# A hybrid attention and mLSTM layer: state products of both directions in one split product, value blocks in pairs

## The chip, the cores and the metric

The kernel runs on one core of one Trainium2 chip. The metric is device time in microseconds (us) of one execution. A core has five engines with queues of their own: PE (TensorE, matrix products), DVE (VectorE), ACT (ScalarE), POOL (GpSimd) and SP (SyncE, which here only issues DMAs). Loading PE's stationary matrix is listed apart as PEld. A queue is worked off in order, so an instruction that waits holds up all that stand behind it on its engine.

## The reference

One layer over T = 2048 tokens of width 1024, in float32. What matters here:

```python
proj = h @ w_in + b_in          # na_q na_k na_v na_z, ml_q ml_k ml_v ml_o ml_z, gates
na_out = neighbourhood_attention(na_q, na_k, na_v, rpb) * silu(na_z)
mq, mk = split(silu(short_conv(concat(ml_q, ml_k))))
# chunked mLSTM, one head, forward (the backward direction is the same on flipped input)
m_new = max(bl_c + m, max(a_c)); decay = exp(bl_c + m - m_new); w = exp(a_c - m_new)
C_new = decay * C + einsum('s,se,sd->ed', w, v_c, k_c)     # state product
n_new = decay * n + einsum('s,sd->d', w, k_c)              # its normaliser
...
y = concat([na_out, ml_out]) @ w_out; out = rmsnorm(x + gate * y)
```

There are 4 mLSTM heads of width 128. The kernel uses 16 chunks of 128 tokens.

## The kernel before

**Split products.** Float32 factors of the large products are written as a high part (rounded to the matrix unit's single-pass format, `F32R`) and a low part, the rest. Three products stand for one: high x high, high x low, low x high. `mm3` (lines 635 to 640) does this over 8 slices of the contraction, so 24 matmuls make one tile. Small products, those of the mLSTM among them, are made in plain float32; the profile shows each as two PE records.

**Stages in order.**
1. `start` (hand-ordered with `manual_schedule`): modulation, normalisation, splitting of h; blocks 0 and 1 of the projection (value and output gate of heads 0 and 1), and the first token group of block 2.
2. `tok_blocks` (775 to 796): blocks 2 and 3 (heads 2 and 3) and 4 and 5 (na_v), each 256 columns wide, over four groups of 512 tokens, a group being four PSUM tiles of 128 tokens (`vo_group`, `nav_group`). The order is block by block. There are two weight slots (`wslot`), used by turns; `raw_w` loads the next block in two halves into `raw0` and `raw1`, ACT copies the high part, DVE makes the low part. After each tile `next(self.chain)` writes one step of the gate chain (`gate_both`, then `decays`), small dependent steps on DVE, ACT and PE. Bias rows lie in two `brows`, one for even and one for odd blocks, loaded by `load_bias`.
3. `conv_blocks` (970): blocks 6 to 9 (ml_k, ml_q) with tokens in the columns, the short convolution on DVE, for k also a transpose on PE (lines 1043 to 1049); results go to `d_ck` in DRAM.
4. `phase1b`: per head `ml_pass1` (state products of the 16 chunks from both ends, and the recurrence `follow`) and `ml_pass2` (outputs). Between their steps `pump(n)` puts n matmuls of the generator `nq_gen` (line 1094: blocks 10 to 17, 512 columns). In `ml_pass1` a chunk is loaded as one `kv` tile (k turned, v, a column of ones), DVE multiplies v and the ones by the chunk's weights for each direction (line 1263), PE makes one 129-column product `dc` for each direction (line 1283), and DVE or ACT takes it up (1267, 1290, 1294). Five pumped matmuls on some steps and four on the others stand between chunks (`PUMP1` = 4.5). `ml_pass2` gathers four chunks in `hm` (two buffers), turns them on PE, multiplies them with the gate tile `zt` in place (`end`, 1405 to 1410) and stores `zt`.
5. `phase2` (hand-ordered): neighbourhood attention patch by patch and the output product (line 1676). Buffers `ring` are cleared by POOL (line 1748), tables are loaded into `tabs` (1557).

**Order.** Outside `start` and the patch loop of `phase2` a planner orders each engine's instructions from the program's order and its own estimate of times; semaphores are set by it. In the hand-ordered parts every engine's order is the program's. SP's is too: in the last round of `start` it issues, in this order, the two halves of block 2's weights, the store of block 0 (line 721), the last two fills `d_t<-big` (758) and the store of block 1 (721); then in `tok_blocks` the loads for the gate row (587, 590, 596), `rneg` and three fills `d_e<-big` (727, 731), the halves of block 3 (203) and its bias row (681).

Of the kernel before, what the change touches and what calls it, by code (L numbers as in the profile page):

```python
# [58 lines left out]
class Kernel:  # L59
# [30 lines left out]
    def scratch(self):  # L90
        d = self.dram
        self.d_vna = d.tile([T, 512], F32, name="d_vna")
        self.d_ck = d.tile([MH, NC, P, 897], F32, name="d_ck")
# [41 lines left out]
    def phase1(self):  # L135
# [14 lines left out]
        wb = self.pool(r1a, "wb", bufs=1, side="right")  # L150
        self.wslot = []
        for nm, pl in (("a", wa), ("b", wb)):
            self.wslot.append(tuple(pl.tile([P, KT, 272 if nm == "a" else 256], F32R, name=f"w{part}_{nm}") for part in ("hi", "lo")))
# [18 lines left out]
        self.tok_blocks(self.pool(toks, "chain", bufs=1, side="right"))  # L172
# [16 lines left out]
    def stage_tile(self, name):  # L189
        self.stages.reverse()  # L190
        return self.stages[1].tile([P, 1032], F32, tag="st", name=name).rearrange("p (o c) -> p o c", o=4)

    def load_w(self, blk, slot, halves=(0, 1)):
        for part in self.raw_w(blk, slot, halves):
            part()

    def raw_w(self, blk, slot, halves=(0, 1)):
        nc = self.nc
        hi, lo = self.wslot[slot]

        def part(half):
# [11 lines left out]

        return [part(half) for half in halves]

    def start(self, left):
# [310 lines left out]
        def next_w():  # L527
            for part in self.raw_w(2, 0):
                yield
                part(nc.vector)  # L530

        fills = self.table_fills()
        self.chain = iter(())
# [132 lines left out]
    def nav_group(self, blk, slot, g):  # L666
        nc = self.nc
        c0 = (blk - 4) * 256
        st = self.stage_tile(f"stv_{blk}_{g}")
        for o in range(4):  # L670
# [3 lines left out]
            next(self.chain, None)  # L674
            if o == 1:
                self.flush()
        dst = self.d_vna[g * GT : (g + 1) * GT, c0 : c0 + 256].rearrange("(o p) c -> p o c", p=P)
        self.defer(lambda: nc.sync.dma_start(dst, st[:, :, :256]))
# [17 lines left out]
    def vo_group(self, h, slot, g, first=None, brow=None, tops=(), stage=None):  # L696
# [5 lines left out]
        for o in range(4):  # L702
# [10 lines left out]
            next(self.chain, None)  # L713
            if o == 1:
                self.flush()
        nc.scalar.activation(st[:, :, 129:257], st[:, :, 129:257], AF.Sigmoid)
        dst = self.d_ck[h, 4 * g : 4 * g + 4, :, 128:385].rearrange("o p c -> p o c")
        if g == 0 and h < 3:
            (nc.scalar if h == 0 else nc.sync).dma_start(dst, st[:, :, 0:257])
        else:  # L720
            self.defer(lambda: nc.sync.dma_start(dst, st[:, :, 0:257]))

# [52 lines left out]
    def tok_blocks(self, chain_pool):  # L775
        self.wide = chain_pool.tile([P, 2 * D], F32, name="wide")
        self.chain = itertools.chain(self.gate_both(chain_pool), self.decays(chain_pool))
        order = [2, 3, 4, 5]
        next(self.chain)
        r = self.tables_begin(chain_pool)  # L780
        for n, blk in enumerate(order):
            parts = self.raw_w(blk + 1, (blk + 1) % 2)
            if blk < 5:
                self.load_bias(blk + 1)
            for g in range(1 if blk == 2 else 0, NG):
                if blk < 4:
                    self.vo_group(blk, blk % 2, g)
                else:
                    self.nav_group(blk, blk % 2, g)
                if g in (1, 2):  # L790
                    parts[g - 1](self.nc.vector)
                if blk == 2 and g == 3:
                    self.tables_bias(r)
# [4 lines left out]
    def gate_chain(self, pool, gates):  # L798
# [29 lines left out]
        nc.scalar.activation(a, a, AF.Ln, bias=1.0)  # L828
        lf = new("lf")
# [78 lines left out]
    def decays(self, pool):  # L908
# [20 lines left out]
        def raised(n):  # L929
# [5 lines left out]
            dst = self.d_ck[h, 4 * gi : 4 * gi + 4, :, 641 + d * CH : 641 + (d + 1) * CH].rearrange("c p t -> p c t")  # L935
# [87 lines left out]
    def conv_group(self, pool, u, kind, ct, g):  # L1023
# [14 lines left out]
        dst = self.d_ck[ct, 4 * g : 4 * g + 4, :, 385 + j * CH : 385 + (j + 1) * CH].rearrange("c p t -> p c t")  # L1038
# [7 lines left out]
        st = self.stage_tile(f"stk_{ct}_{g}")[:, :, 0:128]  # L1046
# [118 lines left out]
    def phase1b(self, left, right):  # L1165
# [30 lines left out]
        mls.close()  # L1196
        self.todo = []
        self.stacks = [pps, right, left]

    def close(self):  # L1200

        self.last_z()
# [258 lines left out]
    def phase2(self):  # L1461
# [405 lines left out]
        with self.tc.manual_schedule():  # L1867
            for m in range(len(patches) + 1):
                slot(m)
# [95 lines left out]
```

## Time and profile before

| | us |
|---|---|
| median of 3 runs (lowest, highest) | 1277.23 (1277.06, 1277.59) |
| the profiled execution | 1276.39 |
| its span, first to last instruction | 1274.5 |
| stage 2, blocks 2 to 5, PE at line 638 | 130.6 to 305.8 of the span |
| stage 3, convolution blocks | 305.8 to 491 |
| the four `ml_pass1`, first to last `dc` | 533 to 555, 625 to 648, 718 to 741, 812 to 834 |
| first table step of the patch loop (line 1598) | 927.96 |

How to read it: a row of a group view gives line, engine, operation, output<-input, shape and count, then busy time and mean duration. A timeline row gives start, duration, engine, line and operation, and in brackets how long the engine was idle before and what ended that. PE's matmuls overlap: a record of a 256-column matmul lasts 0.28 us while the next starts 0.12 us later, so costs on PE are taken from start to start.

### The profile page before, as it was taken

How to read it: one execution, taken by the hardware profiler on the slowest of the kernel's cores; microseconds unless marked ns; L12 is line 12 of the kernel's file. 1: busy time of each engine (PE TensorE's matmuls, PEld its weight loads, DVE VectorE, ACT ScalarE, POOL GpSimd, SP SyncE). 2: the span in 40 equal slices, each digit the busy share in tenths (PEclk: the TensorE clock that was granted, in tenths of full speed). 3: DMA queues.
4: the chain of work that ended last, by engine and by line, in shares of the span. 5: the costliest groups of instructions: out<-in, count | busy, mean ns of one | idle time of the engine just before them, and what ended most of it. 6: DMA issues, size and time to landing. Idle time of an engine off the chain costs nothing.

```text
span 1274.5 us, 22948 instructions
## 1 busy us (share of the span) xinstructions
PE 1264.4 (99%) x8168; PEld 1095.4 (86%) x8168; DVE 790.3 (62%) x2391; ACT 537.7 (42%) x1182; POOL 201.7 (16%) x368
## 2 busy tenths in 40 slices
PE   9999999999999999999999999999999999999997
PEld 8999999999888888888888888888877888888886
DVE  7875542213667664267777778777556766767664
ACT  6642425442334222123323323324357565565552
POOL 0000003440000000000001001000424331332541
PEclk9999999999999999999999999999999999999999
DMA  9999947996678764745757867746677755655551
GB/s 366 335 309 286 283 147 198 249 245 180 180 180 189 165 154 115 207 131 164 204 160 207 251 189 215 240 149 186 207 249 266 230 162 160 203 177 176 176 173 67
DMA packets 217082, 259.08 MB, mean 203 GB/s; under 512 B 23435, under 2 KB 163595, under 8 KB 216968
## 3 DMA queue, kind: packets, MB, share of 16 engines
q1 hardware_dynamic: 149542, 190.09, 52.1%
q0 software_dynamic: 13616, 37.28, 8.9%
q10 hardware_dynamic: 53810, 30.24, 8.4%
q8 instruction: 65, 1.06, 0.3%
q14 instruction: 49, 0.40, 0.1%
HBM read 173.05 MB, written 92.72 MB: 209 GB/s over the span
## 4 chain that ended last, share of the span: by engine, by line
PE 95%; DVE 2%; ACT 1%; issue 1%; DMA 0%; DVEq 0%; ACTq 0%
PE pq L1094 27%; PE y L1676 14%; PE pc L639 5%; PE pc L640 5%; PE pc L638 5%; PE pO L1633 4%; PE pT L1618 3%; PE pvo L638 3%; PE pvo L640 3%; PE pvo L639 3%; PE pS L1587 3%; PE pvo L693 3%; PE pv L640 2%; PE pv L639 2%; PE pv L638 2%; PE pi L1346 2%
## 5 line engine op out<-in xcount | busy, mean ns | idle before, releaser
L1094 PE MATMUL pq<-hhi,whi_a 128*128 128x512 f32 x512 | 208.4, 407 | 0.0
L1094 PE MATMUL pq<-hlo,whi_a 128*128 128x512 f32 x512 | 207.8, 406 | 0.0
L1094 PE MATMUL pq<-hhi,wlo_a 128*128 128x512 f32 x512 | 207.2, 405 | 0.0
L1368 POOL TENSOR_TENSOR hm<-hm,ck 128x128 f32<-128x128 f32 x64 | 28.2, 440 | 580.3 <-DVE hm L1367 541.0
L1094 PEld LDWEIGHTS pq<-hhi,wlo_a 128*128 128x128 f32 x512 | 96.8, 189 | 16.7 <-issue 0.2
L1094 PEld LDWEIGHTS pq<-hlo,whi_a 128*128 128x128 f32 x512 | 96.7, 189 | 16.1 <-issue 0.4
L1094 PEld LDWEIGHTS pq<-hhi,whi_a 128*128 128x128 f32 x512 | 96.8, 189 | 15.9
L1599 ACT ACTIVATE ring<-ring,mn 128x480 f32<-128x480 f32 (+5 forms) x128 | 75.9, 594 | 55.8 <-DVE mn L1598 55.8
L1620 ACT ACTIVATE ring<-pT 96x384 f32<-96x384 f32 (+3 forms) x128 | 65.8, 514 | 63.5 <-PE pT L1618 62.0
L1676 PE MATMUL y<-hhi,wlo_a 128*128 128x512 f32 (+1 forms) x272 | 87.0, 394 | 0.2 <-ACT y L1683 0.2
L1676 PE MATMUL y<-hhi,whi_a 128*128 128x512 f32 x256 | 86.2, 408 | 0.0
L1349 ACT ACTIVATE num<-px,gtile 128x129 f32<-128x129 f32 x120 | 38.7, 367 | 105.2 <-PE px L1344 91.5
L1522 POOL DMA_DIRECT2D v<-d_vna x158 | 78.7, 505 | 15.6 <-issue 4.4
L1618 PEld LDWEIGHTS pT<-ident,ring 128*128 128x128 f32 (+2 forms) x416 | 51.1, 136 | 19.2 <-ACT ring L1620 3.7
L1618 PE MATMUL pT<-ident,ring 128*128 128x128 f32 (+2 forms) x416 | 66.2, 272 | 0.0
L638 PE MATMUL pvo<-whi_b,hhi 128*128 128x256 f32 x224 | 63.6, 284 | 0.0
L1598 DVE CUSTOM_DVE_ANT_0 ring<-pS,tab 128x480 f32<-128x480 f32 (+5 forms) x128 | 61.9, 539 | 2.6 <-PE pS L1587 2.4
L640 PE MATMUL pvo<-whi_b,hlo 128*128 128x256 f32 x224 | 63.1, 282 | 0.0
L639 PE MATMUL pvo<-wlo_b,hhi 128*128 128x256 f32 x224 | 63.0, 281 | 0.0
L934 ACT ACTIVATE dec<-dec,gtile 128x128 f32<-128x128 f32 x128 | 41.3, 391 | 46.9 <-POOL dec L927 43.2
L673 DVE TENSOR_TENSOR stv<-pv,brow 128x256 f32<-128x256 f32 x32 | 13.6, 425 | 71.8 <-PE pv L640 71.8
L710 DVE TENSOR_TENSOR stvo<-pvo,brow 128x256 f32<-128x256 f32 x60 | 24.7, 418 | 50.7 <-PE pvo L640 40.0
(343 smaller groups left out, 3331.3 us busy)
## 6 DMA issues: line engine op xcount, KB each, us to landing
ck<-d_ck SPq DMA_DIRECT2D x64, 384.5 KB, 3.6
rawq<-in_w_main_dram SPq DMA_DIRECT2D x28, 512.0 KB, 5.2
raw<-in_w_main_dram SPq DMA_DIRECT2D x18, 512.0 KB, 6.2
kv<-d_ck SPq DMA_DIRECT2D x64, 128.5 KB, 3.0
dec<-d_mneg SPq DMA_DIRECT2D x32, 256.0 KB, 6.0
d_ck<-dec ACTq DMA_DIRECT2D x32, 256.0 KB, 6.9
qs<-d_qna SPq DMA_DIRECT2D x30, 256.0 KB, 3.9
xr<-in_x_p_dram POOLq DMA_DIRECT2D x15, 512.0 KB, 3.9
```

The costliest lines, as they stand in the source:

```text
L638: nc.tensor.matmul(ps, lhi(k), rhi(k), start=(k == 0), stop=False)
L639: nc.tensor.matmul(ps, lhi(k), rlo(k), start=False, stop=False)
L640: self.mark = nc.tensor.matmul(ps, llo(k), rhi(k), start=False, stop=(k == KT - 1))
L934: nc.scalar.activation(t[:, o, :], t[:, o, :], AF.Exp, bias=self.cols["g"][:, d, h, c : c + 1])
L1094: self.mark = nc.tensor.matmul(patch_ps(ps) if patch else ps, w, self.htok(h, g, k, patch), start=(k == 0 and n == 0), stop=(k == KT - 1 a ...
L1522: queue.dma_start(chunks[key][r * nkc : (r + 1) * nkc, :], rows[r])
L1598: nc.vector.tensor_tensor_reduce(pt[:, :nk], ps, tabs[ct][:, j * nk : (j + 1) * nk], 1.0, 3e38, ALU.add, ALU.min, mn)
L1599: nc.scalar.activation(pt[:, :nk], pt[:, :nk], AF.Exp, bias=mn, scale=-1.0, accum_out=sums[:, j : j + 1])
L1618: nc.tensor.transpose(ps[:cs, i, :], U[u][j][:, i * cs : (i + 1) * cs], self.ident)
L1620: nc.scalar.activation(t[:cs, :nch, :], ps[:cs, :nch, :], AF.Copy)
L1633: nc.tensor.matmul(po[j * HD : (j + 1) * HD, ct, :], v[:n, h * HD : (h + 1) * HD], pt[j][:n, i, :], start=(i == 0), stop=(i == nch - 1))
L1676: nc.tensor.matmul(y, m[:, k, :], w[k][:, cs], start=(k == 4 and n == 0), stop=(k == 3 and n == 2))
```

## The change

- **Pairs.** The weight slots become two halves of one pair of tiles (`wpair`). `pair_group` makes a tile of 512 columns from two value blocks at once. The order of stage 2 becomes (block, group) = (2,1), (3,0), pair (2,2), pair (2,3), (3,1), (4,0), pairs (4,1), (4,2), (4,3), (5,0); a pair is of blocks 2 and 3 or of 4 and 5. Block 3's raw halves are issued in `start`, each right behind the split of block 2's half. The split of a block lies within single groups (`splits`). Two more stage buffers. A pair tile takes two steps of the gate chain. `load_bias(3)` is written behind `tables_begin`.
- **State products.** The convolution stores k turned as a high and a low part (`d_ck` rows of 1025 instead of 897 values). ACT makes the high part of the weighted v, DVE the low part, for both directions side by side; PE makes three products of 258 columns. Chunks at the ends, which need one direction, get both.
- **Places.** The second weight slot stays allocated; `kv` tiles (seven places as before), `zt` and the four tables lie in it (`spare`). `end` writes to `hm` and stores `hm`. Ten `ring` buffers: two `hm` and eight of their own; DVE clears their columns from 256 on at the start of the patch loop. Table 3 is loaded after `close`.

```diff
 def tok_blocks
-        order = [2, 3, 4, 5]
         next(self.chain)
         r = self.tables_begin(chain_pool)
-        for n, blk in enumerate(order):
-            parts = self.raw_w(blk + 1, (blk + 1) % 2)
-            if blk < 5:
-                self.load_bias(blk + 1)
-            for g in range(1 if blk == 2 else 0, NG):
...
-                if g in (1, 2):
-                    parts[g - 1](self.nc.vector)
+        order = [(2, 1), (3, 0), (2, 2), (2, 3), (3, 1), (4, 0), (4, 1), (4, 2), (4, 3), (5, 0)]
+        both = ((2, 2), (2, 3), (4, 1), (4, 2), (4, 3))
+        self.load_bias(3)
+
+        def splits(rest, after):
+            for _ in range(rest):
+                yield
+            for part in self.parts:
+                part(self.nc.vector)
+                yield
+            if after:
+                self.parts = self.raw_w(*after)
+                if after[0] == 5:
+                    self.load_bias(4)
+                if after[0] == 6:
+                    self.load_bias(5)
+
+        turns = {0: (1, (4, 0)), 4: (0, (5, 1)), 5: (0, (6, 0)), 9: (0, None)}
...
 def start, next_w
-            for part in self.raw_w(2, 0):
+            self.parts = []
+            for half, part in enumerate(self.raw_w(2, 0)):
                 yield
                 part(nc.vector)
+                self.parts.append(self.raw_part(3, 1, half))
...
+    def pair_group(self, blk, g):
...
+        for o in range(4):
+            ps = self.pp.tile([P, GT], F32, tag="pp", name=f"p2_{blk}_{g}_{o}")
+            self.mm3(
+                ps.rearrange("p (a c) -> p a c", a=2),
+                lambda k: self.hhi[g][:, k, o * P : (o + 1) * P],
+                lambda k: self.hlo[g][:, k, o * P : (o + 1) * P],
+                lambda k: hi[:, :, k, :256],
+                lambda k: lo[:, :, k, :256],
+            )
+            for j, st in enumerate(sts):
...
+                next(self.chain, None)
+            next(self.mid, None)
...
 def gate_chain
         nc.scalar.activation(a, a, AF.Ln, bias=1.0)
+        yield
...
 def conv_group
-        st = self.stage_tile(f"stk_{ct}_{g}")[:, :, 0:128]
-        nc.scalar.activation(st, ps.rearrange("p (a q) -> p a q", a=4), AF.Copy, scale=KSCALE)
+        nc.scalar.activation(hi.bitcast(F32R), turned, AF.Copy, scale=KSCALE)
+        nc.vector.scalar_tensor_tensor(lo.bitcast(F32R), turned, KSCALE, hi, ALU.mult, ALU.subtract)
...
 def ml_pass1
-            t = tiles[k] = ml.tile([P, 257], F32, tag="kv", bufs=7, name=f"kv_{h}_{order[k]}")
+            half, i = divmod(k % 7, 5)
+            t = tiles[k] = self.spare(half, 1024 * half + 385 * i, 385)
...
-                nc.vector.tensor_scalar(sides[k][d], v, self.cols["w"][:, d, h, c : c + 1], None, ALU.mult)
+            hi, lo = sides[k] = [ml.tile([P, 2, 129], F32R, tag=f"w{e}", bufs=3, name=f"w{e}_{h}_{c}") for e in range(2)]
+            for d in range(2):
+                w = self.cols["w"][:, d, h, c : c + 1]
+                nc.scalar.activation(hi[:, d, :], v, AF.Copy, scale=w)
+                nc.vector.scalar_tensor_tensor(lo[:, d, :], v, w, hi[:, d, :].bitcast(F32), ALU.mult, ALU.subtract)
...
-            for d, w in sorted(sides[k].items()):
-                nc.tensor.matmul(dc[:, d, :129], kt, w, start=True, stop=True)
+            for n, (a, b) in enumerate(((khi, whi), (khi, wlo), (klo, whi))):
+                nc.tensor.matmul(dc, a, b, start=n == 0, stop=n == 2)
...
 def ml_pass2, end
-            nc.vector.scalar_tensor_tensor(z, ps, self.mlw[:, h : h + 1], z, ALU.mult, ALU.mult)
-            src = zt[gi]
+            src = hm[gi]
+            nc.vector.scalar_tensor_tensor(src.rearrange("p a q -> p (a q)"), ps, self.mlw[:, h : h + 1], z, ALU.mult, ALU.mult)
...
 def phase2
-        for t in ring[4:] + ring[:4]:
-            nc.gpsimd.memset(t, 0.0)
...
         with self.tc.manual_schedule():
+            for t in ring:
+                nc.vector.memset(t[:, 256:], 0.0)
```

138 lines of the change are left out of this document (86 added, 52 removed).

## The prediction

> **What bounds the kernel now.** First the page's head and chain of work, then the list of PE's waits.
>
> ```profile
> span 1274.5 us, 22948 instructions
> PE 1264.4 (99%) x8168; PEld 1095.4 (86%) x8168; DVE 790.3 (62%) x2391; ACT 537.7 (42%) x1182; POOL 201.7 (16%) x368
> PE 95%; DVE 2%; ACT 1%; issue 1%; DMA 0%; DVEq 0%; ACTq 0%
> PE pvo L436 <- ACT hhi L404: 1.2, 2, 0.8
> PE y L1676 <- DVE hlo L1569: 0.4, 1, 0.4
> ```
>
> The span lies within the profiled execution of 1276.39 us, itself 0.84 below the median of 1277.23. PE is 95% of the chain that ended last, and hardly ever waits: the longest wait in the list's rows shown is 0.8 us. So only PE time taken out counts, and new work on other engines costs what it makes PE wait.
>
> **The change part by part.** *Pairs.* From start to start of one line's records in a tile of 24:
>
> ```profile
> L638 PE MATMUL pv<-whi_a,hhi x128: 276/280/283, 215.0 to 260.0; 128*128 128x256 f32 x128
> L638 PE MATMUL pc<-hhi,whi_b x64: 390/393/404, 446.7 to 490.7; 128*128 128x512 f32 x64
> 491.53 41.70 PE pq L1094 x180
> 82.94 12.09 PE pvo L693 x96
> ```
>
> Block 4: 127 rounds of three in 45.0 us, 0.1181 each at 256 columns. Block 9: 63 rounds of three in 44.0, 0.2328 at 512; line 1094 gives 41.70/180 = 0.2317. Five pair groups x 4 tiles x 24 = 480 wide matmuls replace 960: 480 x (2 x 0.1181 - 0.2328 or 0.2317) = 1.6 or 2.2 us. I take 1.9. The split operand and columns in two runs are not seen to cost in line 1094's patches either.
>
> *State products.* Around one chunk on PE, and the record counts:
>
> ```profile
> 538.36 0.39 PE L1094 MATMUL pq<-hhi,wlo_a 128*128 128x512 f32 x1
> 538.59 0.38 PE L1283 MATMUL dc<-kv 128*128 128x129 f32 x2
> 538.81 0.39 PE L1283 MATMUL dc<-wv,kv 128*128 128x129 f32 x2
> 538.95 0.48 PE L1094 MATMUL pq<-hhi,whi_a 128*128 128x512 f32 x1
> 539.27 0.39 PE L1094 MATMUL pq<-hlo,whi_a 128*128 128x512 f32 x1
> L1283 PE MATMUL dc<-kv x128: 271/273/276, 533.1 to 834.1; 128*128 128x129 f32 x128
> L1283 PE MATMUL dc<-wv,kv x112: 275/275/276, 535.8 to 834.3; 128*128 128x129 f32 x112
> ```
>
> From 538.36 to 539.27 are 0.91 us with two wide matmuls (0.463) in them: both directions cost 0.447, one 0.223. 240 records are 120 products: 56 chunks with two and 8 with one. No row has 258 columns. Below it stands 256 (0.1181), above it 272 (12.09/96 = 0.1259), so three cost 0.354 to 0.378; by nearness 0.357. Gain 56 x (0.447 - 0.357) = 5.0, less 8 x (0.357 - 0.223) = 1.1: **3.9 us**, with the ends 2.6 and 4.1.
>
> The Trainium skill (TensorE: Matmul & The Clock Gate, Back-to-back issue gap) puts an isolated matmul's gap at N/2.4 + 2.5 ns. By it the pairs would give an estimated 1.2 us and the state products 5.7, and the forecast would be about 1271.8; the rows here show 8 to 10 ns more per matmul, and they decide.
>
> *What the planner must place in `ml_pass1`.*
>
> ```profile
> 648.55 0.47 DVE L1263 TENSOR_SCALAR kv<-kv,gtile 128x129 f32<-128x129 f32 x2
> 649.20 2.19 DVE L1267 SCALAR_TENSOR_TENSOR st<-st,gtile,st 128x129 f32<-128x129 f32 x8
> 658.39 0.63 ACT L1349 ACTIVATE num<-px,gtile 128x129 f32<-128x129 f32 x2 [3.74 <-PE px L1344]
> 718.00:743.00 25.00, 25.00 (x144) 21.56 (x143) 19.16 (x69) 8.93 (x23) 0.41 (x1) 1.00 0.79 224
> ```
>
> Per head DVE exchanges 30 weightings (0.24) for 32 low parts (0.27): 1.6 us more on 19.2 of 25 (the window's third column). ACT gets 32 high parts at some 0.3: 10 on 8.9. Both fit. Weights are made two chunks ahead, 2.8 us of pumped work, against ACT plus DVE of some 1.2. `kv` grows by half, with as many places. I take 0; without that cover it is the fourth rival.
>
> *Convolution, `hm`, patch loop.*
>
> ```profile
> 306.00:399.00 93.00, 93.00 (x427) 75.61 (x427) 61.54 (x123) 30.44 (x46) 0.00 (x0) 1.00 0.74 187
> L1137 DVE SCALAR_TENSOR_TENSOR qst<-pq,bcol,qst x24: 719/744/751, 668.3 to 967.0; 128x512 fp32r<-128x512 f32 x24
> 593.20 0.37 ACTq L1410 DMA_DIRECT2D d_mix<-zt  x1
> 596.08 0.29 DVE L1366 TENSOR_SCALAR hm<-num,r 128x128 f32<-128x128 f32 x1
> 908.02 3.37 POOL L1748 MEMSET ring<- 128x512 f32 x7
> 927.96 0.46 DVE L1598 CUSTOM_DVE_ANT_0 ring<-pS,tab 128x288 f32<-128x288 f32 x1 [2.18 <-PE pS L1587]
> ```
>
> 16 low parts of k at 0.74 are 12 us of DVE in a stretch of 93 of which 62 are taken, under PE's blocks: 0. `hm` is now freed by a store issued at 593.20, 2.9 us before its next write at 596.08; a landing later than that delays DVE, under a whole chunk of pumped work: 0, at worst some 0.5 at each of eight places. Ten half-width clears on DVE, at half of POOL's 3.37/7 some 2.4 us, fall into the 2.18 us that DVE idles before the first table step; PE has pumped work there: 0 to 0.5. Table 3 is wanted second to last: 0. The larger rows of `d_ck` move 8 MB on a queue that is not full in these stages.
>
> *The start of stage 2.* Here the change moves DMAs past each other on SP.
>
> ```profile
> 120.43 0.91 SPq L203 DMA_DIRECT2D raw<-in_w_main_dram  x2
> 122.65 9.32 SPq L758 DMA_DIRECT2D d_t<-big  x2
> 133.05 4.41 SPq L721 DMA_DIRECT2D d_ck<-stvo  x1
> 137.55 0.88 SPq L587 DMA_DIRECT2D cact<-in_small_dram  x1
> 143.05 2.63 SPq L731 DMA_DIRECT2D d_e<-big  x3
> 145.73 1.11 SPq L203 DMA_DIRECT2D raw<-in_w_main_dram  x2
> 127.00:159.00 32.00, 32.00 (x271) 31.59 (x271) 16.89 (x49) 13.38 (x16) 0.32 (x3) 1.00 1.01 285
> 130.63 1.21 DVE L208 TENSOR_TENSOR wlo_a<-raw,whi_a 128x1024 fp32r<-128x1024 f32 x1
> 152.56 1.22 DVE L208 TENSOR_TENSOR wlo_b<-raw,whi_b 128x1024 fp32r<-128x1024 f32 x1 [5.31 <-ACT whi_b L207]
> 151.47 1.06 ACT L207 ACTIVATE whi_b<-raw 128x1024 fp32r<-128x1024 f32 x1 [4.30 <-DMA raw<-in_w_main_dram]
> 143.26 0.21 ACT L588 ACTIVATE cact<-cact 128x8 f32<-128x8 f32 x1 [3.81 <-DMA cact<-in_small_dram]
> 130.63 0.28 PE L638 MATMUL pvo<-whi_a,hhi 128*128 128x256 f32 x1
> ```
>
> Block 3's second raw half can be issued only when block 2's low part is done, 130.63 + 1.21 = 131.84. The fills of line 758, which went out at 122.65, stand behind it now, some 9.6 us later, and all after them with them: block 1's store, `cact`, the gate row, `d_e`, then the bias row of block 3, about where the raw halves stood (145.73). DMA is full there (share 1.01). If only the queue's empty stretch is lost (128 to some 130.5, when the halves of block 2 have landed and nothing follows), the shift is 1.2 us; if the issues take as long as before, 9.6. From issue to use took 5.7 us (145.73 to 151.47). The bias row lands at 145.7 + 5.7 + shift = 152.6 to 161.0. Block 3's first eviction (0.42 on DVE) comes at 145 instead of behind three block 2 groups, and waits for it; DVE's gate chain stands behind. PE goes on into the four PSUM buffers: 130.63 + 8 x 24 x 0.1181 + 0.2 = 153.5. It then waits 0 to 7.9 us. Part of the 9.3 us that the fills held SP was waiting for room in the queue, which is emptier now, so I take a shift of some 3 and a wait of **1.5 us**. Before, DVE stood 5.31 us for the raw half without PE noticing: four buffers do cover a block of that length.
>
> Sum: -1.9 - 3.9 + 1.5 = **-4.3**. 1276.39 - 4.3 = 1272.1 for the profiled execution, **1272.9** beside the median.
>
> **The rivals.** *No wait at all.* The bias row lands by 153: -5.8, 1271.4. For it: most of the shift may vanish in the emptier queue; against it: share 1.01.
> *The bias row is late.* Shift 5 to 9.6, PE waits 3.5 to 7.9, middle 5.7: -0.1, 1277.1. For it: block 1's store took 4.41 us of issue and the fills of line 731 another 2.63, in whatever order.
> *ACT takes `cact` before block 3's high parts* (slower). If the planner puts line 588, which is written first, ahead of the two copies, they wait for `cact`: it lands at 143.3 plus the shift, the first low part is done 2.5 later. PE wants it at 130.63 + 96 x 0.1181 + 0.2 = 142.2, so it waits 3.6 plus the shift. At 5.4 that is 9.0: -5.8 + 9.0 = +3.2, **1280.4**; slower from a wait of 8.4. Against it: the planner placed line 588 behind Exp and Ln before, so it expects `cact` late. The Trainium skill (TensorE: Matmul & The Clock Gate, Architectural detail) calls ACT and DVE strict first-in-first-out queues; so the copy could not pass the waiting line 588, as the sigmoid of block 2 did not before 143.26 here.
> *Weights late in `ml_pass1`.* A split and an eviction on ACT (1.05 + 0.7) ahead of high parts eat the lead; 0.4 us at two splits a head, 8 in all, about 3: -1.3, 1275.9. Against it: ACT is busy 8.9 of 25.
> That the narrow products run slower than their neighbours by columns is held in the bounds.
>
> **How the numbers follow.** Forecast 0.37, no wait 0.23, late bias 0.21, `cact` first 0.14, late weights 0.05. A measurement tells this kernel from no change at about 0.2%, 2.55 us. Forecast and no wait are faster: 0.60; late bias and late weights within: 0.26; `cact` first slower: 0.14. The range runs from 1269.5 (both gains at their upper end, 6.3, and no wait, 1270.9, with a little below) to 1279.5 (bias 7.9 late, +2.1), leaving out most of the slower case.
>
> **What would show it.** Pair tiles 24 x 0.232 = 5.57 us apart; `dc` records of 258 columns 0.119 apart, 192 in all; stage 2 shorter by 1.9 less the wait; a hole on PE at about 153 that ends with a line 710 eviction of block 3 just behind the bias row. A hole at 142 ended by line 208 shows the third rival; waits at line 1283's successors the fourth. The forecast is wrong if PE waits elsewhere for over 2 us, or if 258 columns cost over 0.13 each.

## The result: 1.1% slower, and the profile after

The changed kernel takes 1291.78 us (median of 4 runs, 1291.06 to 1292.87), the kernel before 1277.14 beside it: ratio 1.0113, interval 1.0098 to 1.0128. The forecast was 1272.9 with a range of 1269.5 to 1279.5. It missed in sign and in size.

First the head, the chain of work and the list of PE's waits of the changed kernel.

```profile
span 1289.3 us, 22169 instructions
PE 1265.6 (98%) x7640; PEld 1071.7 (83%) x7640; DVE 805.6 (62%) x2425; ACT 576.5 (45%) x1311; POOL 195.4 (15%) x358
PE 66%; DMA 13%; DVE 3%; issue 2%; ACT 2%; SPq 1%; POOL 1%; ACTq 0%; POOLq 0%; DVEq 0%
PE pc L638 <- ACT whi L207: 4.9, 1, 4.9
PE pvo L639 <- DVE ends L901: 4.3, 1, 4.3
PE kt L1099 <- ACT acc_k L1090: 1.5, 2, 0.8
```

PE was 95% of the chain and is 66% now; DMA came in with 13%. Two waits are over 4 us, where the longest before was 1.1 (`dense`, at the very start, in both kernels). Now stage 2 (from the last product of 272 columns to the first of block 6), the convolution and phase 1b of both, before first. Columns: window, its length, busy time and instructions of PE, PEld, DVE, ACT, POOL, the granted clock, the DMA share, GB/s.

```profile
119.11:305.93 186.82, 186.82 (x1559) 184.15 (x1558) 59.42 (x140) 76.92 (x168) 43.62 (x40) 1.00 0.83 216
305.93:491.36 185.43, 185.43 (x834) 150.68 (x833) 118.59 (x236) 56.47 (x84) 0.00 (x0) 1.00 0.71 171
491.36:927.16 435.80, 435.54 (x2359) 370.47 (x2358) 296.93 (x1097) 146.32 (x330) 41.88 (x91) 1.00 0.65 191
```

```profile
121.98:318.45 196.47, 186.49 (x1079) 161.37 (x1077) 53.42 (x137) 76.51 (x168) 41.43 (x38) 0.99 0.85 196
318.45:507.56 189.11, 187.38 (x832) 151.28 (x833) 127.53 (x250) 56.90 (x84) 0.00 (x0) 0.99 0.81 191
507.56:942.00 434.44, 433.15 (x2312) 366.64 (x2310) 309.39 (x1121) 185.06 (x459) 39.98 (x85) 1.00 0.69 204
```

Stage 1 ends 2.9 us later, stage 2 takes 9.6 more, the convolution 3.7 more, phase 1b 1.4 less, phase 2 is unchanged: together 14.8, the difference of the two spans (1289.3 and 1274.5).

**The hole at 146.** SP, DVE, ACT and PE of the changed kernel, from the timeline (start, length, instruction, idle time before it and what ended it); the first line is the kernel before:

```profile
121.45 1.15 SPq L721 DMA_DIRECT2D d_ck<-stvo  x1
```

```profile
133.36 0.33 SPq L203 DMA_DIRECT2D raw<-in_w_main_dram  x1
133.79 0.38 SPq L721 DMA_DIRECT2D d_ck<-stvo  x1
134.72 0.42 DVE L753 TENSOR_TENSOR stvo<-pvo,brow 128x256 f32<-128x256 f32 x1
141.31 0.43 DVE L753 TENSOR_TENSOR stvo<-pvo,brow 128x256 f32<-128x256 f32 x1 [6.18 <-DMA d_ck<-stvo]
142.36 1.04 ACT L207 ACTIVATE whi<-raw 128x1024 fp32r<-128x1024 f32 x1
146.41 0.28 PE L638 MATMUL pvo<-whi,hhi 128*128 128x256 f32 x1
146.69 0.29 DVE L884 SCALAR_TENSOR_TENSOR wide<-wide 128x128 f32<-128x128 f32 x1 [2.76 <-ACT wide L881]
149.37 0.43 DVE L753 TENSOR_TENSOR stvo<-pvo,brow 128x256 f32<-128x256 f32 x1
149.71 1.22 DVE L208 TENSOR_TENSOR wlo<-raw,whi 128x1024 fp32r<-128x1024 f32 x1
150.98 0.39 PE L639 MATMUL pvo<-wlo,hhi 128*128 128x256 f32 x1 [4.29 <-DVE ends L901]
```

Block 3's first raw load waits on SP until block 2's split has read the buffer (133.36), and block 0's last store waits behind it; before the change that store went out at 121.45. Until it lands, DVE stands 6.18 us for its staging tile (to 141.31). Only then come two evictions (the second at 142.38), the start of the gate chain and the first half of block 3's low part (142.71). The gate chain waits for ACT once more, and the next eviction, at 149.37, and the second half of the low part, at 149.71, stand behind it.

That second half is what PE waits for. PE began block 3's first tile at 144.99; twelve products later, at 146.41, it has used up the first half of the weights. The next record, line 639, reads `wlo`, and it starts 0.05 us after the low part of 149.71 is done (150.93). The list names the copy to `ends` because it ends at the same moment; the product does not read `ends`. The high part that goes with it was ready from 143.40 on. So the low part was late by its place in DVE's queue.

**The hole before the convolution.** ACT, the changed kernel:

```profile
316.93 0.37 ACTq L990 DMA_DIRECT2D d_ck<-dec  x1
317.34 2.00 ACT L207 ACTIVATE whi<-raw 128x1024 fp32r<-128x1024 f32 x2 [0.44 <-ACT dec L988]
313.24 0.28 PE L640 MATMUL pv<-whi,hlo 128*128 128x256 f32 x1
```

The last line is PE's last product of block 5; its first of block 6 is at 318.45, as soon as the first of the two high parts is done (1.1 us after 317.34). Block 6's high parts stand on ACT behind the last of the decay rows' Exp. In the kernel before that Exp ended at 293, and block 6 had been split at 267 to 296, under the four groups of block 5. A pair holds both weight slots, so in the new order block 6's slot comes free only when one group of block 5 (11.3 us) is left.

**The clock behind the holes.** Windows of 4 us of the changed kernel:

```profile
12.00:16.00 4.00, 4.00 (x19) 3.93 (x18) 2.35 (x5) 1.76 (x4) 0.00 (x0) 0.50 1.01 407
152.00:156.00 4.00, 4.00 (x25) 4.00 (x24) 0.01 (x1) 2.88 (x3) 0.10 (x1) 0.64 1.01 289
320.00:324.00 4.00, 4.00 (x14) 3.17 (x14) 1.79 (x3) 0.00 (x0) 0.00 (x0) 0.74 0.98 219
```

After each hole PE is busy all the time at a granted clock of 0.64 and 0.74: some 1.4 and 1.0 us lost within these windows, on top of the hole. The clock records of the trace have it at half for 3.4 us behind each, so some 1.7 us lost each time. The Trainium skill (TensorE: Matmul & The Clock Gate, Part 1: The HAM clock gate) says that an idle window of about 3.4 us halves the clock and a busy one restores it; holes of 4.3 and 4.9 us agree. Shorter holes can cost it here too. From 20 us on, in the traces of all runs, the clock went to half behind each of the 13 holes of 3.1 us and more, behind none of the 19 between 1.0 and 1.95, and behind 6 of the 12 between 2.0 and 2.7. The first line is another matter: at 11.5 the clock fell to half for 6.8 us, and most of stage 1's 2.9 us is that (see the end).

### The profile page after: what moved, and what is told of

It is laid out like the page before. It is cut to its first block, busy times and chain, and to the rows that moved or that the text cites. A ratio compares the mean times of both kernels' runs of the same rounds, so it can differ in the third digit from the quotient of the medians.

```text
span 1289.3 us, 22169 instructions
## 1 busy us (share of the span) xinstructions
PE 1265.6 (98%) x7640; PEld 1071.7 (83%) x7640; DVE 805.6 (62%) x2425; ACT 576.5 (45%) x1311; POOL 195.4 (15%) x358
## 4 chain that ended last, share of the span: by engine, by line
PE 66%; DMA 13%; DVE 3%; issue 2%; ACT 2%; SPq 1%; POOL 1%; ACTq 0%; POOLq 0%; DVEq 0%
PE pq L1151 24%; PE y L1741 14%; PE pO L1698 4%; PE pT L1683 3%; PE pS L1652 3%; DMA d_ck<-dec 3%; PE pc L639 2%; PE pc L638 2%; PE pc L640 2%; DMA wraw<-in_w_out_dram 2%; DMA dec<-d_mneg 2%; PE pi L1411 2%; DMA d_wo<-wraw 2%; PE px L1409 2%; DMA raw<-in_w_main_dram 2%
## 5 line engine op out<-in xcount | busy, mean ns | idle before, releaser
L1151 PE MATMUL pq<-hlo,whi 128*128 128x512 f32 x512 | 206.5, 403 | 0.0
L1151 PE MATMUL pq<-hhi,whi 128*128 128x512 f32 x512 | 206.3, 403 | 0.0
L1151 PE MATMUL pq<-hhi,wlo 128*128 128x512 f32 x512 | 206.0, 402 | 0.0
L1151 PEld LDWEIGHTS pq<-hhi,whi 128*128 128x128 f32 x512 | 96.8, 189 | 16.4
L1151 PEld LDWEIGHTS pq<-hhi,wlo 128*128 128x128 f32 x512 | 96.7, 189 | 16.5 <-issue 0.2
L1151 PEld LDWEIGHTS pq<-hlo,whi 128*128 128x128 f32 x512 | 96.8, 189 | 15.7 <-issue 0.4
L638 PE MATMUL pc<-hhi,whi 128*128 128x512 f32 x256 | 102.6, 401 | 4.9 <-ACT whi L207 4.9
L639 PE MATMUL pc<-hlo,whi 128*128 128x512 f32 x256 | 101.9, 398 | 0.0
L640 PE MATMUL pc<-hhi,wlo 128*128 128x512 f32 x256 | 101.2, 395 | 0.2 <-DVE wlo L208 0.2
L1741 PE MATMUL y<-hhi,wlo 128*128 128x512 f32 (+1 forms) x272 | 87.0, 394 | 0.2 <-ACT y L1748 0.2
```

The lines of the kernel that those rows point to most:

```text
L638: nc.tensor.matmul(ps, lhi(k), rhi(k), start=(k == 0), stop=False)
L639: nc.tensor.matmul(ps, lhi(k), rlo(k), start=False, stop=False)
L640: self.mark = nc.tensor.matmul(ps, llo(k), rhi(k), start=False, stop=(k == KT - 1))
L1151: self.mark = nc.tensor.matmul(patch_ps(ps) if patch else ps, w, self.htok(h, g, k, patch), start=(k == 0 and n == 0), stop=(k == KT - 1 a ...
L1741: nc.tensor.matmul(y, m[:, k, :], w[k][:, cs], start=(k == 4 and n == 0), stop=(k == 3 and n == 2))
```

## The experiments

The runs fall into five groups: e1 to e4, e5 to e8, e9 to e12, e13 to e15, and e16 with e18 and e19. Each group ran on one chip beside the kernel before, and different groups ran on different chips, where the kernel before measured 1276.5, 1276.4, 1276.7, 1276.4 and 1278.2 us. Ratios are to those.

### Which half of the change: e1 and e2

e1 is the changed kernel with stage 2 of the kernel before; e2 keeps the pairs and takes the state products back:

```
- order = [(2, 1), (3, 0), (2, 2), (2, 3), (3, 1), (4, 0), ...]
+ order = [2, 3, 4, 5]
```

```
- for n, (a, b) in enumerate(((khi, whi), (khi, wlo), (klo, whi))):
-     nc.tensor.matmul(dc, a, b, start=n == 0, stop=n == 2)
+ for d, w in sorted(sides.pop(k).items()):
+     nc.tensor.matmul(dc[:, d, :], kt, w, start=True, stop=True)
```

> The changed kernel with the order of groups, the two staging tiles, the raw loads and the gate chain of stage 2 of the kernel before: only the state products (and the split of k) are changed. Theory (the loss sits in the order of stage 2): no hole of PE over 1.5 us; stage 2 as before (175 us from the first product of block 2 group 1 to the first of block 6); phase 1b 1.4 us shorter as in the changed kernel, two waits of some 0.8 us at line 1099's transposes; 1275.0 to 1278.5 us. Rival (the wider rows of the scratch tensor and the doubled load of ACT and DVE slow the whole kernel): over 1285 us.

> The changed kernel with the state products undone: k is stored unsplit and the products are again plain fp32, two directions apart; the pairs and their order stay. Theory: the three holes of PE (4.6 us at about 146, 1.2 at about 234, 5.2 at about 313) and the slow clock behind them are all there; phase 1b back to 435.8 us; 1289 to 1293 us. Rival (the state products cost it): 1274 to 1277 us.

Measured: e1 1283.21 us, ratio 1.0045 (1.0030 to 1.0061); e2 1298.86, ratio 1.0171 (1.0158 to 1.0184). Both lose, and neither expectation held. The order carries most, but e1 should have been at par, and e2 is slower than the whole change: its hole before the convolution is 7.7 us, with the last Exp at 319.0 instead of 316.5. Why its decays end even later is open. e1's stage 2 is as before (187.2), its phase 1b is 0.7 us longer, and PE has new waits:

```profile
PE pvo L731 <- DVE stvo L748: 1.9, 1, 1.9
PE ht L1444 <- ACT hm L1437: 1.4, 2, 1.2
PE kt L1078 <- ACT acc_k L1069: 1.3, 2, 0.9
```

The first is in stage 1 (at 108 us), where the work is that of the kernel before; what differs is the row of the scratch tensor `d_ck` and the place of the weight slots. e7 tests the row alone.

### The two holes: e3, e4, e5, e8

e3 writes block 3's raw loads at the head of stage 2, behind the gate chain's start; e5 writes them one step later in stage 1's last group; e4 copies block 6's high parts on DVE; e8 makes group 1 of blocks 4 and 5 two single groups, block 5's at the end.

```
# e3                                     # e5
- self.parts.append(self.raw_part(...))    parts[0](nc.vector)
...                                        yield
  self.load_bias(3)                      + self.parts.append(self.raw_part(3, 1, 0))
+ self.parts = self.raw_w(3, 1)            parts[1](nc.vector)
# e4                                     # e8
+ if blk == 6:                           - ..., (4, 3), (5, 0)]
+     nc.vector.tensor_copy(hi, raw)     + ..., (4, 3), (5, 0), (5, 1)]   # (4, 1) unpaired
```

> The changed kernel, but the two raw loads of block 3 are written behind the gate chain's start at the head of stage 2 instead of between the splits of block 2, so that they no longer stand ahead of block 1's last but one store on the SP queue. Theory: the store goes out at some 124 instead of 133.8, DVE does not wait 6.2 us for its staging tile, the hole of PE at 146 (4.5 us) and the half clock behind it (1.6 us) go: 1284.5 to 1287 us. Rival (the gate chain with its activation tables between the evictions makes the hole, whenever the store lands): 1290.5 to 1293 us.

> The changed kernel, but the high parts of block 6's weights are copied on DVE instead of ACT, so that they do not stand behind the decay rows' Exp on ACT. Theory: the two splits run at some 302 to 307, PE goes from block 5's group 0 to the convolution without the 5.2 us hole, and the half clock behind it goes: 1283.5 to 1287 us. Rival (the raw weights or the staging tiles are late there, and ACT is only the last of several): 1290 to 1293 us.

> The changed kernel, but in the last group of stage 1 the first raw load of block 3 is written one step later, so that block 0's last store goes to SP ahead of it and does not wait there for block 2's split; the raw loads of block 3 still stand ahead of the fills. Theory (that store holds DVE by its staging tile, DVE holds the evictions and the gate chain): the store goes out by 129 instead of 133.8, DVE's wait of 6.2 us goes, the hole of PE at 146 (4.5 us) and the half clock behind it (1.6 us) go, and with the gate chain some 5 us earlier the decays end earlier and the hole before the convolution gets smaller: 1283 to 1287 us, 2 us more where PE waits at 108 as in the runs with an undisturbed start. Rival (the gate chain between the evictions holds PE by itself): 1290 to 1294 us.

> The changed kernel with group 1 of blocks 4 and 5 as two single groups instead of a pair, block 5's at the end: the high and low parts of block 6 then have two groups (22.7 us) of cover instead of one (11.3). Theory (a pair fills both weight slots, so only the single groups around it cover a swap, and 11.3 us are too little with the decay rows' Exp ahead on ACT until 317): the hole before the convolution goes with the slow clock behind it, the pair lost costs 0.4: 1284 to 1287 us. Rival (the decays just run on with the group added, or the conv stage waits for ACT instead): 1289 to 1293 us.

Measured: e3 1300.19, e4 1293.20, e5 1292.43, e8 1293.40 us. None helped in sum; each came out at its rival's price or above it. In e3 DVE no longer stood for the tile, but block 3's raw loads went out only at 152, and PE waited 2.2 us for its weights and 6.9 for the gate chain. In e4 the hole before the convolution went (stage 2 192.8 instead of 196.5) and came back in the convolution, 195.1 instead of 189.1. Block 7's raw loads went out only at 321.97, behind the decay rows on SP (4.0 us of its wait ended with a decay store); ACT, in its queue's order, stood 9.1 us for them, and the convolution's inputs (line 1054, at 331.59) behind them. They came 16.7 us after the stage's first product, in the kernel before 5.8.

```profile
PE kt L1102 <- ACT acc_k L1093: 4.9, 3, 2.6
PE kt L1102 <- issue: 2.7, 1, 2.7
329.35 1.06 ACT L210 ACTIVATE whi<-raw 128x1024 fp32r<-128x1024 f32 x1 [9.10 <-DMA raw<-in_w_main_dram]
```

e8 did the same (stage 2 195.2 with a group less in pairs, convolution 192.1, whose inputs waited 5.1 us, by the list for a decay row's store). In e5 the store went ahead, the first hole fell from 4.3 to 1.7 us and the half clock behind it went; stage 2 took 194.6. But PE now waited 1.2 us at 162 for an eviction that wants block 3's bias row, and the hole before the convolution grew to 6.1. So the store explains most of the first hole. The second has a root of its own: the decays end too late, wherever block 6's split is put.

### The row of the scratch tensor: e7, e9, e15, e16

The change widens the rows of `d_ck` from 897 to 1025 numbers, 3588 to 4100 bytes. These are the kernel before with nothing but the row changed; in e16 the tensor is as large as with 1025, but its rows lie 897 apart.

```
- self.d_ck = d.tile([MH, NC, P, 897], F32, name="d_ck")
+ self.d_ck = d.tile([MH, NC, P, 1025], F32, name="d_ck")   # e7; e9: 1153; e15: 1024
# e16
+ room = d.tile([MH, NC * P * 1025], F32, name="d_ck")
+ self.d_ck = room[:, : NC * P * 897].rearrange("m (n p c) -> m n p c", n=NC, p=P)
```

> The kernel before with rows of 1025 instead of 897 numbers in the scratch tensor d_ck, and nothing else. Theory (the row's length costs nothing; the hole of PE at 108 in three of the runs comes from another cause): 1276 to 1277.5 us, no hole at 108. Rival (the stores into rows of 4100 bytes take longer beside the fills, and DVE waits for its staging tile at some 103): a hole of about 2 us at 108, 1278 to 1280 us.

> The kernel before with rows of 1153 numbers (4612 bytes) in d_ck, of which 897 are used. The runs with 1025 (4100 bytes) lost 8.9 us by the row alone. Theory (4100 bytes is 4 past 4096, so that the same columns of all partitions' rows lie at nearly the same place modulo 4096, and the stores meet there; a longer row that is no near multiple is harmless): 1275.5 to 1278 us, no hole at 108, no waits over 1 us at the transposes of k. Rival (a longer row, or the tensors that it moves, costs whatever its length): 1281 us or more.

> The kernel before with rows of 1024 numbers (4096 bytes) in d_ck, of which 897 are used. Theory (rows near a multiple of 4096 bytes make the stores slow, not the length): as slow as with 1025, 1281 to 1290 us, waits at 108 and at the transposes of k. Rival (1025 was slow by something else, such as where the tensors behind it come to lie): 1275.5 to 1278 us.

> The kernel before with d_ck as large as with rows of 1025 numbers, so that every tensor behind it lies where it lay in e7_stride, but with its rows 897 apart as before. Theory (the distance of 4100 bytes from row to row makes the stores slow): 1275.5 to 1277.5 us, stores of stvo in stage 2 some 4.1 us from issue to landing. Rival (where the tensors behind d_ck lie makes it): 1281 us or more, stores over 6 us.

Measured: e7 **1285.28 us, ratio 1.0064 (1.0042 to 1.0085)**; e9 1276.57, 0.9995 (0.9987 to 1.0004); e15 1276.64, 1.0002 (0.9993 to 1.0011); e16 1278.34, 0.9999 (0.9990 to 1.0007). One number in the source, no instruction more or less, costs 8.9 us (medians; the interval is 5 to 11). Neither expectation held; the wait at 108 came as the rival had it, the whole cost more. From issue to landing in 130 to 300 us (last column, median us), before, e7 and e9:

```profile
d_ck<-dec ACTq DMA_DIRECT2D x32, 256.0 KB, 6.9
d_ck<-stvo SPq DMA_DIRECT2D x8, 514.0 KB, 4.1
```

```profile
d_ck<-dec ACTq DMA_DIRECT2D x29, 256.0 KB, 7.4
d_ck<-stvo SPq DMA_DIRECT2D x8, 514.0 KB, 6.2
```

```profile
d_ck<-dec ACTq DMA_DIRECT2D x32, 256.0 KB, 7.0
d_ck<-stvo SPq DMA_DIRECT2D x8, 514.0 KB, 4.2
```

The same stores of the same bytes take 2 us longer at 4100; in e15 and e16 `d_ck<-stvo` took 3.4 and 4.1 in the same window. The traces of all the runs sort by the row: the store of k split (`d_ck<-stk`, 512 KB) took 6.2 to 6.6 us in the seven with 1025 and 3.4 to 4.5 in the six with 1152 or 1153. The seven and the six ran on different chips, but the kernel before ran beside e7 on one and took its usual 1276.4. PE feels it where a staging tile is waited for:

```profile
PE kt L1045 <- ACT acc_k L1036: 3.2, 2, 2.4
PE pvo L693 <- DVE stvo L710: 2.2, 2, 2.0
```

In e7 the last Exp of the decays is at 308.5 instead of 292.8; its convolution takes 189.4 us, as the changed kernel's 189.1. The place of the tensors behind `d_ck` is not it (e16), and length as such is not it (e9). My theory that nearness to 4096 bytes does it fell with e15: 4096 itself is harmless. The Trainium skill (DMA: Bandwidth & Descriptors, Latency and other measured facts) knows slow copies for row pitches of large powers of two, from 512 KiB up, and takes channel aliasing as the likely cause; a pitch of 4100 is no such case, and 4096 cost nothing here. Where a row begins within 512 bytes does not set 4100 apart either: 3588, 4100 and 4612 all leave 4. What in 4100 makes it slow stays open; and 1024 and 1153 did not run beside 1025 on one chip.

### The change with another row: e10, e11, e12

e10 is the changed kernel, e11 is e1, e12 is e2, each with rows of 1153.

> The changed kernel with rows of 1153 numbers in d_ck instead of 1025, nothing else. Theory (the row's length is one of two causes, the order of groups the other): d_ck stores land sooner, the waits at 108 and at the transposes of k go, the decays end earlier; the holes at 146 and 313 stay in part: 1280 to 1287 us. Rival 1 (the order and the short swap windows make all of it): 1290 to 1293 us. Rival 2 (the row alone makes all of it): 1271 to 1275 us.

> e1_state_only (state products changed, stage 2 of the kernel before) with rows of 1153 numbers. Theory (the row hid the gain of the products): phase 1b some 434 us or less, conv and start as before: 1272 to 1276 us. Rival (the doubled work of ACT and DVE in the chunks and in the convolution eats the gain by itself): 1277 to 1281 us.

> e2_tok_only (pairs and their order, plain state products) with rows of 1153 numbers. Theory (the order costs by itself: block 0's last store behind the raw loads on SP, and one group of cover for block 6's split): holes at 146 and 313 there, 1284 to 1292 us. Rival (with the stores quick again the order's waits fall under PE's cover): 1274 to 1279 us.

Measured: e10 **1277.26 us, ratio 1.0008 (0.9995 to 1.0020)**; e11 1277.91, 1.0006 (0.9996 to 1.0017); e12 1282.22, 1.0046 (1.0031 to 1.0061). With the row mended the change is at par on this chip, not slower (e18 below, with the same row on another, is 0.5% slower). For e10 and e12 no expectation held: both came out between theory and rival. For e11 the rival did: the products gain nothing without the pairs. Why the pairs alone (e12) lose more than the pairs with the products is open. e10's windows (as above) and its longest wait:

```profile
119.01:308.37 189.36, 186.03 (x1079) 161.36 (x1078) 56.18 (x140) 77.59 (x168) 41.46 (x38) 0.99 0.79 207
308.37:493.39 185.02, 185.02 (x834) 150.68 (x833) 124.74 (x247) 56.47 (x83) 0.00 (x0) 1.00 0.72 191
493.39:927.55 434.16, 432.71 (x2311) 366.70 (x2310) 309.16 (x1121) 184.94 (x459) 39.50 (x85) 1.00 0.69 204
PE pvo L639 <- DVE ends L901: 3.3, 1, 3.3
```

The convolution is back at 185.0, though DVE has 6 us more to do there; the hole before it is gone, since the decays end at 304; the hole of the store (3.3) is left; it too ends with the second half of block 3's low part (145.78 to 147.00, PE at 147.04). Of the pairs' and products' gain only 1.6 us in phase 1b shows.

### What is left of the gain: e6, e13, e14, e18, e19

e6 is e1 without the low parts of the weighted values. e13 is e10 with e5's store order; e14 is e13 with the weighted high parts made on POOL, e18 is e13 with one direction's low part made there; e19 is e13 with rows of 1152.

```
# e6
- nc.vector.scalar_tensor_tensor(lo[:, d, :], v, w, hi[:, d, :].bitcast(F32), ALU.mult, ALU.subtract)
# e14
- nc.scalar.activation(hi[:, d, :], v, AF.Copy, scale=w)
+ nc.gpsimd.tensor_scalar(hi[:, d, :], v, w, None, ALU.mult)
# e18, direction 1
+ nc.gpsimd.tensor_scalar(vw, v, w, None, ALU.mult)
+ nc.gpsimd.tensor_tensor(lo[:, d, :], vw, hi[:, d, :].bitcast(F32), ALU.subtract)
```

> As e1_state_only, but the low part of the weighted values is not worked out: the high part stands in its place in the three products, so PE has the same work and DVE 128 instructions of some 0.27 us fewer in the passes over the chunks. Theory (the 3.8 us that PE saves in the products go into waits for DVE, which is over 80% busy there): the waits of PE at lines 1325, 1388, 1437 and 1173 go, phase 1b takes 432 to 434 us instead of 436.5, the whole 1278.5 to 1281 us. Rival (ACT's high parts or the loads of the longer rows hold PE): phase 1b as in e1_state_only, 1282 to 1284.5 us.

> The changed kernel with rows of 1153 numbers and with block 0's last store ahead of block 3's raw loads on SP (as in e5_raw3_first). With the row mended e10_after_1153 has one hole of PE left over 1 us (3.6 at 143.4, half clock behind it). Theory (DVE stands 5.1 us there for the staging tile of that store): the store goes out some 5 us sooner, the hole and the slow clock go: stage 2 (last product of 272 columns to first of block 6) 184 to 186 us instead of 189.4, the whole 1271.5 to 1274.5 us. Rival (the gate chain with its table loads holds the evictions however early the store lands): 1276 to 1278 us.

> As e13_store_first_1153, with the high parts of the weighted values made on POOL instead of ACT. Theory (ACT, which has some 16.6 us of work in each 25 us pass instead of 8.9, lets PE wait at the transposes of hm and takes from the 3.8 us that the products save): phase 1b 432.5 to 433.5 us instead of 434.2, the whole 0.7 to 1.7 us below e13_store_first_1153. Rival (POOL is slower for one instruction, so that DVE's low parts are late): phase 1b over 434.2 us.

> As e13_store_first_1153, with the low part of one of the two directions made on POOL (a product and a subtraction) instead of DVE: 64 fewer instructions of 0.35 us on DVE. Theory (DVE, over 80% busy in the passes, takes back the products' gain: the waits at hm's transposes stand behind its mu): phase 1b 432.5 to 434.2 us, 1273 to 1276 us. Rival (POOL's two instructions for each chunk come too late or slow DVE): phase 1b 435 us or more, 1276.5 us or more.

> As e13_store_first_1153 with rows of 1152 numbers (4608 bytes, a multiple of 64) instead of 1153. With rows of 1024 the kernel before stored d_ck sooner than with 897 (k: 2.6 instead of 3.9 us). Theory (a row whose start is aligned takes the stores out of the way without the loss of 4100): stores of k and of stvo sooner than in e13_store_first_1153 by 0.7 us or more, the hole at 147.9 (1.6 us) under 1 us: 1273.5 to 1276 us. Rival (the stores are no longer what PE waits for): stage 2 as in e13_store_first_1153, 1276 to 1278.5 us.

Measured: e6 1280.72 (phase 1b 434.5 instead of e1's 436.5); e13 1278.86, ratio 1.0007 (0.9996 to 1.0017); e14 1277.56, 1.0011 (0.9999 to 1.0024); e18 1285.22, 1.0047 (1.0032 to 1.0062); e19 1287.74, 1.0077 (1.0064 to 1.0090).

e13's stage 2 came out as expected, 185.9 us, 0.9 under the kernel before (the whole came out above both expectations); the store goes out at 125.81 and DVE waits only for PE:

```profile
125.81 0.38 SPq L725 DMA_DIRECT2D d_ck<-stvo  x1
138.01 0.42 DVE L757 TENSOR_TENSOR stvo<-pvo,brow 128x256 f32<-128x256 f32 x1 [2.44 <-PE pvo L644]
145.19 0.29 DVE L888 SCALAR_TENSOR_TENSOR wide<-wide 128x128 f32<-128x128 f32 x1 [2.64 <-ACT wide L885]
```

The last row is what remains of that hole (1.6 us of PE from start to start): the gate chain waits for ACT, and the second half of block 3's low part stands behind it (148.21). ACT loads a table of 1.28 us ahead of each of the chain's two activations. The whole did not get faster: phase 1b took 435.8, and block 0's first product came 4.8 us later than in the kernel before, behind a clock of 0.50 from 12 to 16.

e6 took 1.9 us less in phase 1b than e1. Relief of ACT (e14, phase 1b 435.9) or of half of DVE's low parts (e18, 435.6) did not bring e13's 435.8 down. Neither reading is firm: the changed kernel, e3, e4, e5, e8, e10, e13 and e19 have the same phase 1b in the source, and it took from 434.2 (e10) to 436.4 us (e8). So what one profile each says about 1 to 2 us there is not shown. e14 and e18 came out as their rivals had it; e19 came out above both of its expectations. e18 and e19, on the chip where the kernel before takes 1278.2, show the second hole again, with rows of 1153, which cost the kernel before nothing (e9), and of 1152, which it was not run with. e19's waits and ACT's order there:

```profile
PE pc L642 <- ACT whi L207: 4.9, 1, 4.9
PE pvo L643 <- DVE ends L905: 2.3, 1, 2.3
311.94 0.37 ACTq L994 DMA_DIRECT2D d_ck<-dec  x1
312.35 2.00 ACT L207 ACTIVATE whi<-raw 128x1024 fp32r<-128x1024 f32 x2 [0.44 <-ACT dec L992]
```

Last Exp and first product of block 6, in us: after 316.5 and 318.5, e5 317.5 and 319.4, e19 311.5 and 313.5, e18 309.6 and 311.5, e13 306.8 and 309.3, e10 303.6 and 308.4. In the first four PE starts block 6 about 2 us behind the start of the last Exp, just when the first of the two high parts is done; in e13 and e10 PE has no hole there. In e10 that high part is done some 3 us before PE wants it. The new order has no room for a decay chain some microseconds late, from whatever cause. No version beat the kernel before.

## Why the prediction was wrong, step by step

- **"The larger rows of `d_ck` move 8 MB on a queue that is not full": the step that failed most.** I counted bytes, and the cost was in the distance between rows. Alone it is 8.9 us (e7); of the 7.8 in its profiled run 2.9 are in stage 1, 0.5 in stage 2, 4.0 in the convolution. In the changed kernel it also made the decays late: their last Exp ends at 316.9, with 1153 at 303.9 (e10). With that row the ratio falls from 1.0113 to 1.0008, some 13 of the 14.6 us lost, as far as two chips can be compared. The "0" in the sum stood on bytes and on the room in the queue; no row of a trace was read for the row's length. None of the rivals held it.
- **A pair fills both weight slots.** The working priced the pairs on PE alone and did not ask what covers the swap of the weights: 45 us for block 6 before, 11.3 after, behind the decays on ACT. 4.9 us and the slow clock behind it. The row of ACT's order was there to be read. The hole comes only with late decays: in e10 it is gone.
- **The start of stage 2: right place, wrong wait.** SP did stand for block 2's split, until 133.36, and block 3's bias row did go out late, at 155.55 instead of 146.88, a shift of 8.7 us within the 1.2 to 9.6. DVE waited for it:

```profile
155.55 0.36 SPq L724 DMA_DIRECT2D brow<-in_b_row_dram  x1
160.62 0.76 DVE L753 TENSOR_TENSOR stvo<-pvo,brow 128x256 f32<-128x256 f32 x2 [2.24 <-DMA brow<-in_b_row_dram]
```

  PE did not feel it here, since it was late already; in e5, with the first hole smaller, it cost PE 1.2 us, near the 1.5 taken. But the working let PE run on until the PSUM buffers are full, to 153.5. PE stopped at 146.41, for the second half of block 3's low part. That part was priced as before, where three groups of block 2 came ahead of block 3's first product and DVE's 5.31 us of standing for it cost nothing; in the new order one group does, and the low part stands in DVE's queue behind the evictions and the gate chain. So "four buffers do cover a block of that length" answered another question. What held the queue up was block 0's last store, which the list of things behind the raw loads missed: 4.3 us and the clock.

  A hole ended by line 208 is the picture of the rival with `cact`, which would have been at 142. Its order did come: ACT took line 588 at 134.72, ahead of block 3's high parts at 139.45 and 142.36. But the load went out at 124.69, ahead of all this, so nothing waited for it; the weights were late on DVE, not on ACT. (The sigmoid that the prediction names as held by line 588 in the kernel before shows no such thing: ACT stood 1.77 us more, until 145.24, for the eviction of 144.76 that it needs.)
- **The clock** was not in the sum. The two holes cost another 1.7 us each, half of the 3.4 that the clock then stood at half; my 7.9 us bound left that out.
- **State products: PE's price was right, the stage's was not.** Three products take 0.360 us in a chunk (median of 60) where 0.357 was taken, so PE does save about 3.9. But phase 1b changed by +0.6 (e8) to -1.6 us (e10) with the pairs in and grew by 0.7 to 0.8 without them (e1, e11). "Both fit" read the busy time (DVE 19.2 of 25). PE's waits at the transposes of `hm` grew from 0.2 to between 0.9 and 2.9 us in all. That single instructions in DVE's or ACT's queue hold PE there, behind more work than before, would fit; the tests of it (e6, e14, e18) lie within what phase 1b varies by, so where the gain goes is open.
- **Pairs:** wide products are 0.232 apart as forecast. e13's stage 2 is 0.9 shorter with a hole of 1.6 in it, of which 0.1 is the product's own, so some 2.4 by subtraction, near the 1.6 to 2.2. The "8 to 10 ns more per matmul" hold for the rows of 256 and 272 columns; by the same reckoning those of 512 are 16 to 17 ns over.
- **Convolution, ring, `hm`:** 0 was right once the rows were mended (185.0 in e10); nothing was seen of the ring or of the z tiles.

With 1153 the sum would have been -4.3 and e10 gave +0.08%, no difference that can be told, with an interval of -0.05 to +0.20% that leaves out the -0.34% of the sum: even there the forecast erred, by the store's hole with its clock and by what phase 1b kept.

## What to carry to other kernels

Changing the row length of a scratch tensor in DRAM is a change of its own: time it alone, with the kernel otherwise untouched, before judging what it was widened for. Where an edit widens a product so that it needs two buffers at once, work out for each refill how long the buffer is free and which queue its refill stands in; PE's time saved is the smaller part. A gain on a bound engine counts only as far as the engines that feed it have room at that moment, and a hole on PE can be paid a second time in clock: here each of 3.1 us and more was, half of those from 2.0 to 2.7, none under 1.95. Where a wait's named releaser is not among what the waiting instruction reads, look for what else ended at that moment.

## What the runs showed of the hardware that was not expected

- Stores of 128 rows at a distance of 4100 bytes took 6.2 us where they took 4.1 at 3588 and 4.2 at 4612. At 4096 the stores of k landed sooner than at 3588 (median, last column; e15 first):

```profile
d_ck<-stk SPq DMA_DIRECT2D x16, 256.0 KB, 2.6
```

```profile
d_ck<-stk SPq DMA_DIRECT2D x16, 256.0 KB, 3.9
```

- Half the clock came behind holes on PE of as little as 2.0 us (e3, e6), and did not behind one of 2.7 (e4). It lasted 3.4 us or a multiple of it, up to 13.7 (e3).
- The clock varies from run to run of one kernel: of 29 runs of the kernel before on one chip, 6 had a mean clock of 0.996 and took 1278.7 to 1279.5 us, the other 23 had 0.997 to 0.999 and took 1275.6 to 1277.1. A loss of that size is in the changed kernel's profile (first product of block 0 at 16.94 instead of 14.57, behind the half clock at 12 to 16), though PE's work up to there is the same. That the six runs lost it at the start too is not shown; only their mean clock is on record.
- The kernel before differed by 0.15% between chips; the new order with e5's store order was at +0.07% on one (e13) and, on the one where the kernel before is slowest, at +0.8% with rows of 1152 (e19) and at +0.5% with rows of 1153 and a low part on POOL (e18). On that chip the stores `d_vna<-stv` between 130 and 300 us took 8.6 us in e16, and 6.5 and 6.8 in the kernel before and e9. So slower transfers there fit, but e13 itself did not run on it: chip and edit are not told apart.
